# Two hybrid attention layers: latent norms folded into weights and evictions, panels reordered, modulation moved out of the first panels

## The chip, the core and the metric

The kernel runs on one core of a Trainium2 chip. The core has a matrix engine (TensorE, in the profile PE for matmuls and PEld for weight loads), VectorE (DVE), ScalarE (ACT), GpSimd (POOL) and SyncE (SP, which here only issues transfers). The metric is the device time of one execution in microseconds (us), the median of several runs. Less is better.

## The reference, cut to what matters

512 latent tokens and 256 context tokens pass through two layers of width 1024. Layer 0 has two groups of heads with one input projection: eight multi-head latent attention heads and eight neighbourhood attention heads. Layer 1 has sliding-window attention. Each layer ends in a SwiGLU. What the change touches is in layer 0: the modulated input, the projection, and the latent heads' norms and up-projections.

```python
def rms_norm(x, gain=None):
    xf = x.astype(jnp.float32)
    y = xf * lax.rsqrt(jnp.mean(xf * xf, axis=-1, keepdims=True) + EPS)
    if gain is not None:
        y = y * gain.astype(jnp.float32)
    return y.astype(x.dtype)
...
    def queries(p, rotate):
        q = rms_norm(p[..., :MLA_Q_RANK], q_norm) @ w_q_up
        q = q.reshape(p.shape[0], p.shape[1], MLA_HEADS, MLA_NOPE + MLA_ROPE)
        q_nope, q_rope = q[..., :MLA_NOPE], q[..., MLA_NOPE:]
        if rotate:
            q_rope = axial_rope(q_rope, rows, cols)
        return jnp.einsum('bshn,hcn->bshc', q_nope, w_uk), q_rope

    def keys(p, rotate):
        c_kv = rms_norm(p[..., MLA_Q_RANK:MLA_Q_RANK + MLA_KV_RANK], kv_norm)
        k_rope = p[..., MLA_Q_RANK + MLA_KV_RANK:][:, :, None, :]
...
    def attend(q_lat, q_rope, c_kv, k_rope):
        sc = jnp.einsum('bqhc,bkc->bhqk', q_lat, c_kv) + jnp.einsum('bqhr,bkr->bhqk', q_rope, k_rope)
        p = jax.nn.softmax(sc.astype(jnp.float32) * scale, axis=-1).astype(c_kv.dtype)
        return jnp.einsum('bhqk,bkc->bqhc', p, c_kv)
```

The query latent has rank 256 (two tiles of 128 features), the key and value latent rank 128 (one tile), the rotated key 32 features. Besides, every layer needs six modulation vectors for each of the two streams: the product of a conditioning vector with a 1024 x 6144 matrix.

## The kernel before, in words

Activations lie with features on the 128 partitions and the 768 tokens (512 latent, `LATS`, then 256 context, `CTXS`) along the free axis. Every fp32 matmul is made of three in a rounded format: operands are split into a high part and a remainder (`split`, lines 303 to 309; `load_w`, lines 268 to 275, for weights: L273 is the high part on ScalarE, L274 the remainder on VectorE or GpSimd), and `mm3` (L283 to L285) adds high x high, high x low, low x high.

Layer 0's mixer goes in this order:

- **Start.** The input is normed and modulated, and the value columns of the neighbourhood heads are projected by `start_products` (through `three`, L696 to L698) into six banks of PSUM at once; `put_vs` empties them by 24 small copies (L418 on VectorE, L419 on ScalarE, by turns).
- **First pair's panels.** `projections(pair_panels(0), PG)` computes queries and keys of the first pair of neighbourhood heads: two weight panels of 1024 x 128, each in 8 steps. Results go to whichever of seven banks comes next (`PG`). Between the steps, `bg` takes one modulation step for every second panel step (`DBG = 0.5`), so eight in all. Here `dense[0]` is true, and a modulation tile is done as L204 and L208 on VectorE for the latent stream, and for the context stream as L221 on GpSimd, L222 on ScalarE and L224 and L225 on VectorE. Outside such stretches both streams are done on VectorE (L233, L235).
- **Neighbourhood jobs** (`na_jobs`, run by `attend`): four pairs of heads, three jobs each. A job computes scores (L680, L681), takes row minima with the bias (L490), exponentials (L486), transposes by TensorE (L427), copies (L418, L419) and weighted sums (L480). `finish_pair` (L405 to L410) divides by the sums. Beside the jobs runs a queue of side steps. `STEPS[0] = (6, 8, 14, 5)` is the number of side steps offered in each job of pair 0, 1, 2, 3; `BG[0]` is the number of modulation steps in each job (one everywhere). The side queue first holds `later_panels`: pair 1, pair 2, latent 0, pair 3, latents 1 and 2, rotated key, eight steps each panel, 80 in all; the remainders of these panels' weights are made on GpSimd. Results go to the two banks "d" (`PQ`).
- Before the last pair's jobs the queue is drained, then `latent_norms` (`gained`, lines 785 to 821) and `mla_prepare` join it, 15 steps. `gained` squares the three latent tiles on GpSimd (L795), adds the two query tiles' squares on VectorE (L799), sums over features by TensorE against a column of ones (L802), takes the root on ScalarE (L805) and the reciprocal on VectorE (L806), builds a diagonal matrix (L810), broadcasts it by TensorE against ones (L814) into a row factor in SBUF (L815), scales each latent tile by gain and factor (L818) and splits it. `mla_prepare` loads three up-projection weights (keys and values, rotated queries, plain queries), and makes the up-projections; their evictions are plain copies on ScalarE (L673; `put_rope` and `rope`, L386 and L781, for the rotated queries).
- `latent_operands(h)` builds what head h's scores read: a cleared tile (L946, GpSimd), the rotated key copied in (L949), high part (L952, ScalarE) and remainder (L953, GpSimd), and the rotated query by a transfer.
- **Latent jobs** (`mla_jobs`): eight heads, two jobs each; beside them the up-projections of pairs 1 to 3 and their values, and one modulation step in each job.

The order of instructions on an engine is fixed before the run by a scheduler that takes program order, priorities (side steps stand back by `lower[0]`) and free buffers. Tiles named "p" share eight buffers (score tiles, temporaries, and the latents), "wr" three (weights being loaded, and every fourth score tile), "wh" and "wl" three each.

Of the kernel before, what the change touches and what calls it, by code (L numbers as in the profile page):

```python
# [41 lines left out]
EV = "dr"  # L42
# [7 lines left out]
DBG = 0.5  # L50
# [3 lines left out]
SQ = 1  # L54
# [8 lines left out]
BG = ((1, 1, 1, 1, 1), 4, (1, 0), (0, 0))  # L63
FIRST = 2000
STEPS = ((6, 8, 14, 5), 5, 3)
# [20 lines left out]
def hybrid_kernel(ctx: ExitStack, tc, I, out):  # L86
# [295 lines left out]
    def rope(dst, src, tabs, swap, scale=1.0, tag="b", eng=None):  # L382
# [3 lines left out]
        S.activation(x[:p, LATS], src, AF.Copy, scale=scale)  # L386
# [4 lines left out]
        eng.tensor_tensor(dst, x[:p, LATS], y[:p, LATS], op=ALU.add)  # L391

# [278 lines left out]
    def put(t, rows=P, scale=1.0):  # L671
        def use(src, c):
            S.activation(t[:rows, c], src, AF.Copy, scale=scale)  # L673

        return use
# [100 lines left out]
    def put_rope(t, tabs, swap, rows=P, scale=1.0, tag="b", eng=None):  # L776
        def use(src, c):
            if c is LATS:
                rope(t[:rows, c], src, tabs, swap, scale, tag, eng)
            else:  # L780
                S.activation(t[:rows, c], src, AF.Copy, scale=scale)  # L781

        return use

    def gained(groups):

        d, m = PQ(), NT // P
        n = m * len(groups)
        col = T("sm", [P, 6, 2]).rearrange("p a b -> p (a b)")[:, :n]
        for i, (tiles, _) in enumerate(groups):  # L790
            acc = None
            for t in tiles:
                s = B()
                if SQ:
                    G.tensor_tensor(s, t, t, op=ALU.mult)  # L795
                else:
                    S.activation(s, t, AF.Square)
                if acc is not None:
                    V.tensor_tensor(s, s, acc, op=ALU.add)  # L799
                acc = s  # L800
            for j in range(m):
                PE.matmul(d[:, i * m + j : i * m + j + 1], acc[:, j * P : (j + 1) * P], ones[:, :1], start=True, stop=True)  # L802
        for i, (tiles, _) in enumerate(groups):
            c = slice(i * m, i * m + m)
            S.activation(col[:, c], d[:, c], AF.Sqrt, bias=eps, scale=1.0 / (P * len(tiles)))  # L805
        V.reciprocal(col, col)  # L806
        yield
        for i, (tiles, g0) in enumerate(groups):
            diag, r = B(), B()
            V.tensor_tensor(diag.rearrange("p (a b) -> p a b", b=P), ident.unsqueeze(1).to_broadcast([P, m, P]),  # L810
                            col[:, i * m : i * m + m].unsqueeze(2).to_broadcast([P, m, P]), op=ALU.mult)
            for c in (LATS, CTXS):
                d = PQ()
                PE.matmul(d[:, : c.stop - c.start], ones, diag[:, c], start=True, stop=True)  # L814
                S.copy(r[:, c], d[:, : c.stop - c.start])  # L815
            res = []
            for j, t in enumerate(tiles):
                V.scalar_tensor_tensor(t, t, gains[:, g0 + j : g0 + j + 1], r, op0=ALU.mult, op1=ALU.mult)  # L818
                res.append(split(t, V))
            groups[i] = res  # L820
            yield
# [3 lines left out]
    ON, lat_raw, kr = [], [None] * 3, []  # L825
# [16 lines left out]
    def projections(panels, get):  # L842

        load = lambda x: load_w(x[0], KT, x[1], G if get is PQ else None)
# [6 lines left out]
    def later_panels():  # L851

        def latent(i):
            def use():
                lat_raw[i] = B(tag="p")
                return put(lat_raw[i])
# [16 lines left out]
        return [*pair(1), *pair(2), latent(0), *pair(3), latent(1), latent(2), (I["w_kr"], 32, rotated)]  # L873
# [20 lines left out]
    def latent_norms():  # L894
        groups = [(lat_raw[2:], 2), (lat_raw[:2], 0)]
        yield from gained(groups)
        wu["ckv"], wu["cq"] = groups

# [415 lines left out]
```

## Time and profile before

| | |
|---|---|
| median of 3 runs | 1696.11 us (1693.7 to 1699.89) |
| profiled execution, its own time | 1700.12 us |
| its span, first to last instruction | 1698.3 us |
| mean granted TensorE clock | 0.972 |
| chain that ended last, by engine | PE 83%, DVE 8%, issue 3%, POOL 2%, ACT 1%, DMA 1% |

The profile is one execution. A line such as `L273 ACT CAST wh<-wr` names the source line, engine, operation, and the tiles written and read; behind the bar stand busy time, mean duration in ns, and how long the engine sat idle before such instructions and for whom. A window's row gives the busy time of each engine with the number of instructions, the granted clock, the share of the transfer engines and the rate. Matmul ends are modelled, so a matmul's own duration overlaps the next; the number of matmuls in a stretch tells the pace.

### The profile page before, as it was taken

To read this page: it belongs to the slowest core of one execution; us is meant where nothing else is said; L and a number is where in the kernel's file an instruction comes from. 1 tells how busy PE (TensorE), PEld (TensorE's weight loads), DVE (VectorE), ACT (ScalarE), POOL (GpSimd) and SP (SyncE) were. 2 spreads that over 40 slices of the span, in tenths; PEclk is the share of its full clock that TensorE was granted. 3 is DMA by queue.
4 is the path that set the end of the run, shared out by engine and by line. 5 is a ranking of instruction groups with operands and counts; after the bars stand their busy time and mean duration, and the time that the engine had idled before them with its cause. 6 is when DMAs were issued, how large, how long until landed. Compare 5 with 4: busy or idle time off the path is not lost.

```text
span 1698.3 us, 24504 instructions
## 1 busy us (share of the span) xinstructions
PE 1609.6 (95%) x9442; PEld 1353.6 (80%) x9442; DVE 972.6 (57%) x2012; ACT 671.5 (40%) x1292; POOL 312.3 (18%) x214
## 2 busy tenths in 40 slices
PE   5989987998998999999999999899999999999997
PEld 3678865776687888888888888787879888888887
DVE  4755335879578854664564424678877533343435
ACT  5455334676345431321221223457755422222223
POOL 0322132230153421310000003376003000000002
PEclk8989987999999999999999999899999999999998
DMA  9415321212532432442453213322005223232322
GB/s 344 144 59 160 102 88 56 66 48 77 203 131 99 156 97 84 137 155 87 150 168 113 81 49 118 105 87 88 1 2 175 87 80 119 83 104 81 116 65 88
DMA packets 73228, 180.44 MB, mean 106 GB/s; under 512 B 9108, under 2 KB 13464, under 8 KB 73112
## 3 DMA queue, kind: packets, MB, share of 16 engines
q1 hardware_dynamic: 71960, 177.83, 31.7%
q8 instruction: 74, 1.21, 0.3%
q10 hardware_dynamic: 1152, 1.05, 0.2%
q14 instruction: 42, 0.34, 0.1%
HBM read 170.72 MB, written 4.19 MB: 103 GB/s over the span
## 4 chain that ended last, share of the span: by engine, by line
PE 83%; DVE 8%; issue 3%; POOL 2%; ACT 1%; DMA 1%; SPq 0%; DVEq 0%; POOLq 0%; ACTq 0%
PE pss L283 9%; PE pss L284 9%; PE pss L285 9%; PE psd L283 8%; PE psd L285 8%; PE psd L284 8%; PE pst L285 6%; PE pst L283 6%; PE pst L284 6%; PE pso L480 5%; PE pst L427 3%; PE pss L680 1%; PE pss L681 1%; PE psd L427 1%; DVE p L490 1%
## 5 line engine op out<-in xcount | busy, mean ns | idle before, releaser
L273 ACT CAST wh<-wr 128x1024 fp32r<-128x1024 f32 (+2 forms) x209 | 200.4, 961 | 482.1 <-PE pss L284 158.0
L274 DVE TENSOR_TENSOR wl<-wr,wh 128x1024 fp32r<-128x1024 f32 (+2 forms) x180 | 212.1, 1179 | 170.8 <-ACT wh L273 168.1
L284 PE MATMUL psd<-b,wh 128*128 128x512 f32 (+3 forms) x644 | 226.3, 351 | 0.0
L285 PE MATMUL psd<-b,wl 128*128 128x512 f32 (+2 forms) x604 | 215.1, 356 | 6.4 <-DVE wl L274 6.4
L283 PE MATMUL psd<-b,wh 128*128 128x512 f32 (+2 forms) x604 | 217.6, 361 | 1.4 <-ACT b L386 1.4
L284 PE MATMUL pss<-b,wh 128*128 128x512 f32 (+1 forms) x564 | 193.5, 344 | 0.0
L283 PE MATMUL pss<-b,wh 128*128 128x512 f32 (+1 forms) x516 | 180.5, 351 | 9.9 <-ACT b L419 8.2
L318 POOL TENSOR_TENSOR p<-p,p 128x256 f32<-128x256 f32 (+1 forms) x42 | 45.5, 1084 | 776.4 <-ACT p L315 773.4
L285 PE MATMUL pss<-b,wl 128*128 128x512 f32 (+1 forms) x516 | 179.6, 348 | 0.0
L284 PE MATMUL pst<-b,wh 128*128 128x512 f32 (+1 forms) x392 | 134.4, 343 | 1.0 <-DVE b L352 0.9
L284 PEld LDWEIGHTS psd<-b,wh 128*128 128x128 f32 (+1 forms) x644 | 122.1, 190 | 16.3 <-issue 0.7
L285 PEld LDWEIGHTS psd<-b,wl 128*128 128x128 f32 (+1 forms) x604 | 114.3, 189 | 23.7 <-DVE wl L274 7.2
L283 PEld LDWEIGHTS psd<-b,wh 128*128 128x128 f32 (+1 forms) x604 | 114.6, 190 | 19.4 <-ACT b L386 1.7
L283 PE MATMUL pst<-b,wh 128*128 128x512 f32 (+1 forms) x352 | 122.8, 350 | 2.3 <-ACT wh L273 2.3
L285 PE MATMUL pst<-b,wl 128*128 128x512 f32 (+1 forms) x352 | 122.8, 349 | 1.1 <-DVE wl L274 1.1
L486 ACT ACTIVATE p<-p,sm 128x512 f32<-128x512 f32 (+3 forms) x144 | 105.1, 730 | 35.4 <-DVE sm L490 35.1
L284 PEld LDWEIGHTS pss<-b,wh 128*128 128x128 f32 x564 | 109.2, 194 | 11.5
L283 PEld LDWEIGHTS pss<-b,wh 128*128 128x128 f32 x516 | 100.1, 194 | 22.9 <-ACT b L419 8.6
L285 PEld LDWEIGHTS pss<-b,wl 128*128 128x128 f32 x516 | 100.1, 194 | 11.7
L283 PE MATMUL pss<-st,wh 128*128 128x512 f32 (+1 forms) x286 | 100.1, 350 | 1.9 <-ACT st L307 1.4
L285 PE MATMUL pss<-st,wl 128*128 128x512 f32 (+1 forms) x286 | 99.4, 348 | 0.1
L221 POOL TENSOR_TENSOR ph<-ph,cond 128x512 f32<-128x512 f32 x28 | 47.6, 1699 | 280.0 <-DVE mod L204 215.0
(276 smaller groups left out, 3672.1 us busy)
## 6 DMA issues: line engine op xcount, KB each, us to landing
wr<-in_w_gu_dram SPq DMA_DIRECT2D x88, 512.0 KB, 3.5
wr<-in_w_out_dram SPq DMA_DIRECT2D x32, 512.0 KB, 3.8
ph<-in_mod_w_dram SPq DMA_DIRECT2D x60, 256.0 KB, 4.0
pl<-in_mod_w_dram SPq DMA_DIRECT2D x60, 256.0 KB, 3.8
wr<-in_w_dn_dram SPq DMA_DIRECT2D x40, 320.0 KB, 2.9
wr<-in_w_dn_dram SPq DMA_DIRECT2D x32, 384.0 KB, 3.1
wr<-in_w_in_dram SPq DMA_DIRECT2D x21, 512.0 KB, 3.7
nb<-in_nb_dram SPq DMA_DIRECT2D x16, 384.0 KB, 3.5
```

The source lines that it names most:

```text
L221: G.tensor_tensor(w, w, cond[:, 1, c], op=ALU.mult)
L273: S.copy(h, r)
L274: (G if eng else V).tensor_tensor(lo, r, f(h), op=ALU.subtract)
L283: PE.matmul(o, wh[:, k], mh[:, c], start=first and k == 0, stop=False)
L284: PE.matmul(o, wh[:, k], ml[:, c], start=False, stop=False)
L285: PE.matmul(o, wl[:, k], mh[:, c], start=False, stop=last and k == n - 1)
L318: (eng or V).tensor_tensor(acc[:, :n], acc[:, :n], t[:, :n], op=ALU.add)
L427: ins = PE.transpose(o[:, i * P : (i + 1) * P], b, ident)
L480: ins = PE.matmul(o[64 * i : 64 * i + 64, c], v(kt), t, start=n == 0, stop=n == len(moving[i]) - 1)
L486: S.activation(p[:, c], p[:, c], AF.Exp, bias=nm, scale=-1.0, accum_out=dn)
L490: V.tensor_tensor_reduce(out=p[:, c], in0=s, in1=bias, op0=ALU.add, op1=ALU.min, scale=-1.0, scalar=start, accum_out=nm)
L680: PE.matmul(o, x, ks[0][:, keys], start=True, stop=False)
```

## The change

1. **Norms.** The gain of each latent feature is multiplied into the up-projection weights as they are loaded (`load_gained`: the high part on ScalarE with a scale, the remainder on VectorE). The latents are split unscaled. Their squares are made by ScalarE from the same bank as the latent itself; `factors` builds the row factor once for the key and value latent and once for the query latent, and the evictions of the up-projections multiply by it on VectorE (`scaled`, and in `values` by the factor as a column).
2. **Order.** The later panels come as pairs 1, 2, 3, rotated key, latent 2, latent 0, latent 1. `mla_prepare` stands in the side queue right behind them, without a drain, in 14 steps. `STEPS[0]` becomes (7, 9, 11, 6).
3. **Modulation.** No modulation step is taken beside the first pair's panels; jobs of the first three pairs take two each instead of one.
4. **Engines.** The later panels' weight remainders, and for the first two latent heads the remainders ("l") and the clearing of tiles ("z"), move from GpSimd to VectorE.

```diff
-EV = "dr"
+EV = "dlrz"
-DBG = 0.5
-SQ = 1
-BG = ((1, 1, 1, 1, 1), 4, (1, 0), (0, 0))
+BG = ((2, 2, 2, 1, 1), 4, (1, 0), (0, 0))
-STEPS = ((6, 8, 14, 5), 5, 3)
+STEPS = ((7, 9, 11, 6), 5, 3)
...
         x, y = B(tag=tag), B(tag=tag)
-        S.activation(x[:p, LATS], src, AF.Copy, scale=scale)
+        scaled(x, src, LATS, scale)
...
+    def scaled(t, src, c, scale):
+
+        p = src.shape[0]
+        if isinstance(scale, float):
+            S.activation(t[:p, c], src, AF.Copy, scale=scale)
+        else:
+            V.tensor_tensor(t[:p, c], src, scale[:p, c], op=ALU.mult)
...
-    def gained(groups):
+    def factors(square, nfeat, scale):
 
         d, m = PQ(), NT // P
...
+        for j in range(m):
+            PE.matmul(d[:, j : j + 1], square[:, j * P : (j + 1) * P], ones[:, :1], start=True, stop=True)
+        S.activation(col, d[:, :m], AF.Sqrt, bias=eps, scale=1.0 / nfeat)
         V.reciprocal(col, col)
...
+        diag, r = B(), B(tag="p")
+        V.tensor_tensor(diag.rearrange("p (a b) -> p a b", b=P), ident.unsqueeze(1).to_broadcast([P, m, P]),
+                        col.unsqueeze(2).to_broadcast([P, m, P]), op=ALU.mult)
+        for c in (LATS, CTXS):
+            d = PQ()
+            PE.matmul(d[:, : c.stop - c.start], ones, diag[:, c], start=True, stop=True)
+            S.activation(r[:, c], d[:, : c.stop - c.start], AF.Copy, scale=scale)
+        return col, r
+
+    def load_gained(src, m, gain):
+
+        r, h, lo = T("wr", [P, 2 * m]), T("wh", [P, 2 * m], F32R), T("wl", [P, 2 * m], F32R)
+        dma(r, src)
+        for k in range(2):
+            c, g = slice(k * m, k * m + m), gains[:, gain[k] : gain[k] + 1]
+            S.activation(h[:, c], r[:, c], AF.Copy, scale=g)
+            V.scalar_tensor_tensor(lo[:, c], r[:, c], g, f(h[:, c]), op0=ALU.mult, op1=ALU.subtract)
+        return tuple(x.rearrange("p (k m) -> p k m", k=2) for x in (h, lo))
...
-        load = lambda x: load_w(x[0], KT, x[1], G if get is PQ else None)
+        load = lambda x: load_w(x[0], KT, x[1])
...
             def use():
-                lat_raw[i] = B(tag="p")
-                return put(lat_raw[i])
+                lat[i], square = (B(tag="b" if i == 1 else "p") for _ in range(2))
+
+                def put(src, c):
+                    S.copy(lat[i][:, c], src)
+                    S.activation(square[:, c], src, AF.Square)
+                    if i == 1:
+                        V.tensor_tensor(squares[0][:, c], squares[0][:, c], square[:, c], op=ALU.add)
+
+                squares[i] = square
+                return put
...
-        return [*pair(1), *pair(2), latent(0), *pair(3), latent(1), latent(2), (I["w_kr"], 32, rotated)]
+        return [*pair(1), *pair(2), *pair(3), (I["w_kr"], 32, rotated), latent(2), latent(0), latent(1)]
...
     def mla_prepare():
-        wu["kv"] = load_w(I["w_ukv"], 2, 512, G)
-        w = load_w(I["w_qr"], 2, 256, G)
-        wu["qn"] = load_w(I["w_qn"], 2, 512, G)
+        wu["kv"] = load_gained(I["w_ukv"], 512, (2, 2))
+        w = load_gained(I["w_qr"], 256, (0, 1))
+        wu["qn"] = load_gained(I["w_qn"], 512, (0, 1))
+        wu["rk"] = factors(squares[2], P, 1.0)
+        yield
+        wu["rq"] = factors(squares[0], 2 * P, MLA_SCALE)
+        yield
+        wu["ckv"] = [split(lat[2], V)]
+        wu["cq"] = [split(lat[0], V), split(lat[1], V)]
+        yield
         KR.extend(split(kr[0][:32, :NT], V))
-        yield
-        yield from pair_ups(0)
         for i in range(2):
             t = B()
-            yield from up(cut(w, i * P, P), wu["cq"], put_rope(t, rope0, SWAP8, scale=MLA_SCALE, eng=V if "r" in EV and i == 0 else None))
+            yield from up(cut(w, i * P, P), wu["cq"], put_rope(t, rope0, SWAP8, scale=wu["rq"][1], eng=V if "r" in EV and i == 0 else None))
             QR.append(split(t, V))
             if i == 0:
+                yield from pair_ups(0, False)
                 ready.append(latent_operands(0))
-
-    def pair_ups(p):
+        yield from values(0)
+
+    def pair_ups(p, also=True):
         kn.append(B())
         qn.append(B())
         wk = wu["kv"]
-        yield from up(cut((wk[0][:, 0:1], wk[1][:, 0:1]), p * P, P), wu["ckv"], put(kn[p]))
-        yield from up(cut(wu["qn"], p * P, P), wu["cq"], put(qn[p], scale=MLA_SCALE))
-        if p % 2 == VP:
+        yield from up(cut((wk[0][:, 0:1], wk[1][:, 0:1]), p * P, P), wu["ckv"], put(kn[p], scale=wu["rk"][1]))
+        yield from up(cut(wu["qn"], p * P, P), wu["cq"], put(qn[p], scale=wu["rq"][1]))
+        if also and p % 2 == VP:
             yield from values(p - VP)
...
-                copy(VM[p + j][:, t * P : (t + 2) * P].rearrange("p (t c) -> p t c", c=P),
-                     o.rearrange("p (t j c) -> p t j c", t=2, j=2)[:, :, j])
+                V.tensor_tensor(VM[p + j][:, t * P : (t + 2) * P].rearrange("p (t c) -> p t c", c=P),
+                                o.rearrange("p (t j c) -> p t j c", t=2, j=2)[:, :, j],
+                                wu["rk"][0][:, t : t + 2].unsqueeze(2).to_broadcast([P, 2, P]), op=ALU.mult)
...
                 lower[0] = L3
-                drain()
-                beside(latent_norms())
-                beside(mla_prepare())
...
-    i = 0
     for _ in projections(pair_panels(0), PG):
-        i += 1
-        bg(int(i * DBG) - int(i * DBG - DBG))
+        pass
     dense[0] = False
     beside(projections(later_panels(), PQ))
+    beside(mla_prepare())
     attend(na_jobs())
```

44 lines of the change are left out of this document (4 added, 40 removed).

## The prediction

> **What bounds the kernel now.** I read the page first: the totals, then the slices of the span.
>
> ```profile
> span 1698.3 us, 24504 instructions
> PE 1609.6 (95%) x9442; PEld 1353.6 (80%) x9442; DVE 972.6 (57%) x2012; ACT 671.5 (40%) x1292; POOL 312.3 (18%) x214
> ...
> PE   5989987998998999999999999899999999999997
> ...
> PEclk8989987999999999999999999899999999999998
> ```
>
> TensorE is the engine that sets the time. The change only touches the first quarter of the span, and there the slices (42.5 us each) show two places where TensorE is less busy and granted a lower clock: the third slice (85 to 127 us) and the sixth and seventh (212 to 297 us). The first slice is the start, which the change leaves alone. So I next asked for the busy time by stage: the end of the start products, the first pair's panels, the neighbourhood jobs with panels beside them, the stretch where the latents are normed, and the latent-attention jobs. Columns: TensorE, weight loads, VectorE, ScalarE, GpSimd busy (instructions), granted clock, DMA share, GB/s.
>
> ```profile
> 58.00:76.00 18.00, 17.49 (x83) 13.89 (x83) 17.04 (x31) 9.96 (x21) 7.24 (x5) 1.00 0.43 138
> 76.00:95.00 19.00, 10.80 (x50) 9.48 (x49) 17.52 (x42) 6.33 (x18) 13.48 (x11) 0.73 0.25 84
> 100.00:226.00 126.00, 124.96 (x852) 106.83 (x852) 57.37 (x145) 60.91 (x138) 22.05 (x13) 1.00 0.38 116
> 226.00:312.00 86.00, 70.19 (x408) 50.57 (x407) 47.97 (x92) 35.71 (x79) 25.05 (x18) 0.80 0.20 64
> 312.00:412.00 100.00, 96.97 (x690) 75.39 (x689) 84.55 (x242) 70.08 (x157) 24.37 (x14) 1.00 0.15 48
> ```
>
> Matmuls per time tell more than busy time. The jobs at 100 to 226 us issue one per 148 ns, the latent jobs at 312 to 412 us one per 145 ns, the valley at 226 to 312 us one per 211 ns with the clock at 0.80. In the panels' stretch, 50 matmuls take 19 us (380 ns each) where the stretch before needs 217 ns for matmuls of the same width. These two stretches are all that the change can win.
>
> **The first pair's panels.** The chain of waits runs over VectorE here; the waits of TensorE in 58 to 100 us have one large entry, and VectorE's groups in 58 to 95 us show what stood in its queue.
>
> ```profile
> PE pss L283 <- ACT b L419: 8.2, 1, 8.2
> ```
> ```profile
> L208 DVE SCALAR_TENSOR_TENSOR mod<-mod,modb 128x1 f32<-128x1 f32 x4 | 3.8, 956 | 0.0
> ...
> L233 DVE CUSTOM_DVE_ANT_0 pl<-wr,cond 128x1024 bf16<-128x1024 f32 x2 | 3.5, 1754 | 0.0
> L274 DVE TENSOR_TENSOR wl<-wr,wh 128x1024 fp32r<-128x1024 f32 x2 | 3.3, 1653 | 0.0
> L204 DVE CUSTOM_DVE_ANT_0 p<-pl,cond,mod 128x512 bf16<-128x512 f32 x4 | 3.0, 738 | 0.0
> L204 DVE CUSTOM_DVE_ANT_0 p<-ph,cond 128x512 bf16<-128x512 f32 x4 | 2.7, 680 | 0.0
> L418 DVE COPY b<-pss 128x128 f32<-128x128 f32 x8 | 2.0, 276 | 0.0
> L224 DVE TENSOR_TENSOR mod<-part,part 128x1 f32<-128x1 f32 x4 | 1.9, 474 | 0.0
> ```
>
> TensorE waits 8.2 us for a panel's bank: all banks still hold value products, and the copies that empty them (L418, L419) queue behind the eight modulation steps (four tiles, both vectors). Without these, L208, both L204 groups and L224 go: 3.8 + 3.0 + 2.7 + 1.9 = 11.4 us out of 34.6 us of VectorE's work in 58 to 95 us, and eight GpSimd products with them. The wait of 8.2 us is shorter than the 11.4 us that leave ahead of it. At 217 ns the 50 matmuls need 10.8 us instead of 19, a gain of 8.2, which also contains the lost clock (0.73). What could eat it: the L233 pair in this list is the first jobs' modulation, already put here; each of these jobs now draws two steps, so two more may come (two at 1.75 us, 3.5 us). So this term lies between 5 and 9; I take 8, nearest the wait that it removes.
>
> **The valley.** Its waits of TensorE, then VectorE's groups of 226 to 312 us, and three pieces of the timeline:
>
> ```profile
> PE pss L680 <- DVE sm L490: 4.7, 1, 4.7
> PE pst L409 <- DVE b L410: 4.2, 1, 4.2
> ```
> ```profile
> L949 DVE CAST st<-b 32x768 fp32r<-32x768 f32 x4 | 8.0, 2036 | 0.1
> L799 DVE TENSOR_TENSOR b<-b,b 128x768 f32<-128x768 f32 x1 | 5.0, 4951 | 0.0
> ...
> L818 DVE SCALAR_TENSOR_TENSOR p<-p,mla_gain,b 128x768 f32<-128x768 f32 x3 | 3.0, 1015 | 5.5 <-ACT b L815 5.5
> L308 DVE TENSOR_TENSOR b<-p,b 128x768 fp32r<-128x768 f32 x3 | 2.9, 958 | 0.9 <-ACT b L307 0.9
> L410 DVE TENSOR_TENSOR b<-b,pst 128x512 f32<-128x512 f32 x4 | 2.8, 688 | 3.5 <-PE pst L409 3.5
> ...
> L810 DVE TENSOR_TENSOR b<-ident_r,sm 128x768 f32<-128x768 f32 x2 | 1.9, 954 | 0.0
> ...
> L410 DVE TENSOR_TENSOR b<-b,pst 128x256 f32<-128x256 f32 x3 | 1.3, 418 | 2.6 <-PE pst L409 2.6
> ```
> ```profile
> 234.38 4.95 DVE L799 TENSOR_TENSOR b<-b,b 128x768 f32<-128x768 f32 x1
> ...
> 273.83 1.02 DVE L949 CAST st<-b 32x768 fp32r<-32x768 f32 x2
> ...
> 281.49 6.98 DVE L949 CAST st<-b 32x768 fp32r<-32x768 f32 x2
> ```
> ```profile
> 236.18 2.33 POOL L274 TENSOR_TENSOR wl<-wr,wh 128x1024 fp32r<-128x1024 f32 x1
> ...
> 283.22 2.76 POOL L946 MEMSET st<- 32x768 f32 x4
> 286.06 4.10 POOL L953 TENSOR_TENSOR st<-b,st 64x768 fp32r<-64x768 f32 x2
> ```
>
> Two things are late. First, one VectorE sum takes 4.95 us where another of its form (L308) takes 0.96, and two casts take 6.98 us where two others took 1.02; beside both runs GpSimd work. TensorE's two waits, 4.2 and 4.7 us, end behind exactly these. The Trainium skill (SBUF — State Buffer, Who interferes with whom) says that VectorE and GpSimd share one port pair, held by one instruction while the other fully blocks; these rows agree. The change takes the work off GpSimd here: squares are made by ScalarE as a panel's bank is emptied, weight remainders (L274) by VectorE, the first pair's remainders and the clearing of tiles (L953, L946) by VectorE.
>
> Second, the order. Now all panels are drained, then the norms run as a chain (squares, sum, reciprocal root, diagonal, broadcast, scaling L818, split L308), and only then the first up-projections. So TensorE has only attention to do, and the clock falls. After the change the latents are split unscaled, the up-projections need no norm, and only their evictions wait for the factor. The counts fit: panels take 80 steps, and 3 x 7 + 3 x 9 + 3 x 11 = 81 are given before the last pair's jobs; preparing takes 14 steps, of which 13 fall among 18 offered in the last three jobs (before: 15 of 15). TensorE's work is the same.
>
> At the latent jobs' 145 ns the valley's 408 matmuls need 59 us: a gain of 27 is the upper end. The lower end is the two waits, 4.2 + 4.7 = 9: contention gone, order worth nothing. Against the upper end stand two factor chains that are now built separately:
>
> ```profile
> L805 ACT ACT_TABLE_LOAD x1 | 1.3, 1283 | 0.0
> ...
> L815 ACT COPY b<-psd 128x512 f32<-128x512 f32 x2 | 1.2, 585 | 4.3 <-PE psd L814 4.3
> ```
>
> Each holds a table load (1.28), the diagonal (L810, 0.95) and the broadcast's eviction (0.59): 2.8 us, 5.6 for both if nothing covers them. While an eviction waits on VectorE, the score minima and copies queued behind it wait, and TensorE for its bank. So I take 27 - 5 = 22. A rule that speaks against the change: the Trainium skill (ScalarE: Activation LUTs, What ACT_TABLE_LOAD costs) adds a drain, 2.66 us for each switch; the trace here shows 1.28 for the load. By it two bare chains would cost 8.4 instead of 5.6 and the valley's gain would be 19.
>
> **What is added elsewhere.** Nine panels' remainders move from GpSimd to VectorE, and nine more modulation steps fall in the first nine jobs:
>
> ```profile
> L274 POOL TENSOR_TENSOR wl<-wr,wh 128x1024 fp32r<-128x1024 f32 x8 | 19.1, 2387 | 91.1 <-ACT wh L273 59.9 <-PE pss L680 31.1
> ```
> ```profile
> L233 DVE CUSTOM_DVE_ANT_0 pl<-wr,cond 128x1024 bf16<-128x1024 f32 x6 | 7.6, 1272 | 2.5 <-DMA wr<-in_mod_w_dram 2.5
> ```
> ```profile
> L274 DVE TENSOR_TENSOR wl<-wr,wh 128x1024 fp32r<-128x1024 f32 (+2 forms) x180 | 212.1, 1179 | 170.8 <-ACT wh L273 168.1
> ```
>
> That is 9 x 1.27 + 9 x 1.18 = 22 us for VectorE, whose 57.4 us of 126 become about 79: TensorE, busy 125 of 126, still hides it. The bound is the 2.5 us that such a step already waits for its weights on SyncE's queue; three buffers of that kind serve panels, modulation and every fourth score tile. I take 0.
>
> In the latent jobs, twelve evictions (six of 512, six of 256 columns) go from ScalarE to VectorE. The nearest row is L410, also a product that reads a bank: 6 x 0.69 + 6 x 0.42 = 6.6 us on an engine busy 84.55 of 100. That gives about 91 beside TensorE's 97. Cover is thin: between 0 and 6.6, I take 3. A gain is excluded: the busier engine takes work from the less busy one.
>
> Sum: -8 - 22 + 0 + 3 = -27 us against the profiled execution's own 1700.12, so 1673. The median is 1696.11, 4 below it; the forecast is 1696 - 27 = 1669.
>
> **The rivals.** (1) The valley is the last pair's own latency: three jobs with light steps beside them cannot fill TensorE whatever the order of the norms. Then the valley gives only what the later stages take back, and the panels' 8 less 3 remain: 1691. For it: the attention's own matmuls are all that fills the valley. Against it: the latent jobs have the same kind of chain and run at 145 ns. (2) Slower: score tiles. Pool "p" has 8 buffers. The change keeps the rotated key, two latents and two squares there, and then two factor tiles until the last up-projection. Latent jobs in flight hold two and four score tiles, of which at least one is elsewhere, so five of the six left. If one more were missing, a job's scores could not start before the previous job's transposes, and sixteen jobs would each show their softmax:
>
> ```profile
> L490 DVE CUSTOM_DVE_ANT_0 p<-pss,zeros,sm 128x512 f32<-128x512 f32 x23 | 16.9, 745 | 7.6 <-PE pss L964 7.6
> ...
> L418 DVE COPY ph<-pst 128x512 f32<-128x512 f32 x14 | 9.4, 683 | 0.4 <-PE pst L427 0.3
> ```
> ```profile
> L486 ACT ACTIVATE p<-p,sm 128x768 f32<-128x768 f32 (+1 forms) x37 | 28.5, 771 | 8.7 <-DVE sm L490 8.6
> ```
>
> 0.75 + 0.77 + 0.68 = 2.2 us, twice for the two halves of a tile's scores: up to 4.4 x 16 = 70, at half of that 35, against 27 gained: 1704 to 1739, say 1715. It decides from the seventh live tile on. (3) The modulation does not leave: its steps, now in the jobs, are put ahead of the value copies as the L233 pair is. Then the first term is 0 to 3 and VectorE stays the bound there: 1696 - 22 + 3 = 1677, or 1674 with 3. With the valley at its lower end as well, 1690.
>
> **How the numbers follow.** A measurement of this kernel tells 0.5% (8.5 us) from no change. Forecast as written: 0.60. Third rival, still faster: 0.16, of which 0.04 lands within 8.5 us. First rival: 0.12, a quarter of it faster by more. Second: 0.12, of which 0.03 is hidden enough to land within 0.5%. So faster 0.60 + 0.12 + 0.03 = 0.75, same 0.04 + 0.09 + 0.03 = 0.16, slower 0.09. Low end: -9 - 27 + 0 = -36, 1660, and 4 for stretched VectorE work that also ends elsewhere: 1656. High end: the first rival, 1691. Outside lie the second rival and a part of the first, under 0.2.
>
> **What would show it.** Right: no wait of TensorE over 2 us before 95 us, clock 1.00 there; the summed squares and the casts near 1 us; the valley's matmuls at about 160 ns and its clock above 0.9; VectorE near 90% in the latent jobs. Wrong: a stretch after the last panel still at half clock, TensorE waiting on evictions of the up-projections, or latent jobs longer than 106 us.

## The result, and the profile after

The changed kernel takes 1673.45 us (median of 4 runs, 1673.07 to 1675.31); the kernel before, measured beside it, took 1695.49. The ratio is 0.9868, with a 95% interval of 0.9848 to 0.9889: 22 us less. The profiled execution took 1673.2 us (span 1671.4, mean clock 0.979).

First the page of the changed kernel: totals, and the slices of TensorE and of its clock.

```profile
span 1671.4 us, 24451 instructions
...
PE 1599.5 (96%) x9442; PEld 1345.7 (81%) x9442; DVE 983.1 (59%) x2056; ACT 661.8 (40%) x1259; POOL 248.2 (15%) x178
...
PE   5999998999999999999999999899999999999997
...
PEclk8999997999999999999999999999999999999999
```

The dip in the third slice is gone; the sixth and seventh, once 8 and 7, are 9 and 8, and the clock of the seventh is still 7. Next the stages, with the prediction's bounds (engine columns as there: TensorE, weight loads, VectorE, ScalarE, GpSimd, clock, DMA share, GB/s).

```profile
58.00:76.00 18.00, 17.52 (x84) 13.90 (x83) 12.71 (x25) 7.53 (x13) 0.00 (x0) 1.00 0.39 137
76.00:95.00 19.00, 19.00 (x108) 16.69 (x107) 12.74 (x34) 7.57 (x17) 4.34 (x6) 1.00 0.25 85
100.00:226.00 126.00, 123.96 (x847) 103.35 (x847) 70.66 (x167) 59.46 (x139) 4.62 (x5) 0.99 0.46 144
226.00:312.00 86.00, 72.33 (x452) 54.12 (x450) 65.98 (x161) 44.27 (x91) 10.01 (x6) 0.86 0.20 62
312.00:412.00 100.00, 96.34 (x660) 72.02 (x661) 88.83 (x242) 62.01 (x136) 17.78 (x9) 0.97 0.22 74
```

The second row is what was hoped for: 108 matmuls where 50 were, at full clock. The fourth is not. The valley has 452 matmuls instead of 408, one per 190 ns instead of 211, and a clock of 0.86 instead of 0.80; the prediction expected 160 ns and over 0.9. At the latent jobs' 145 ns, 452 matmuls would take 65.5 us, so 20.5 us are still lost there, against 26.8 before. The valley gave 6 us of the 22 that were forecast.

So the time must have come from elsewhere too. The trace tells where, by events that both kernels have: the first score of the neighbourhood jobs starts at 99.2 us instead of 108.9 (9.6 earlier); the last latent weighted sum ends at 426.2 instead of 442.4 (16.1 earlier, so 6.5 more); the first SiLU of layer 0's SwiGLU, with the load of its table, starts at 514.3 instead of 535.1 (20.8 earlier, so 4.7 more). These last 4.7 us lie in the output projection, which the prediction didn't speak of. Behind that point the code is the same, and both kernels need 487.6 us from the first to the last SiLU of layer 0. Layer 1, with the same code, took 669.5 us after the change and 675.6 before it; over all kernels of this study it spreads from 669 to 676. At least a part of that is no edit's doing: e10, shown below, has the changed kernel's order of instructions in layer 1 on all four engines, and took 673.0. The profiled execution before was 4.6 us above its median, so the 26.9 us between the two spans are more than the change gave; 20.8 agrees with the 22 of the medians.

What is late in the valley now? TensorE's waits in 226 to 312 us:

```profile
PE pst L411 <- DVE ph L424: 3.1, 1, 3.1
PE psd L174 <- DVE b L397: 2.2, 1, 2.2
...
PE psd L804 <- DVE b L800: 0.9, 1, 0.9
PE psd L281 <- DVE b L397: 0.8, 1, 0.8
```

All four lines shown end behind VectorE, two that are left out between them (1.0 and 0.9 us) behind ScalarE. L397 is the eviction times the factor, L800 the diagonal of `factors`; L424 is a copy, and the timeline of VectorE shows what stood ahead of it:

```profile
267.33 1.50 DVE L953 MEMSET st<- 32x768 f32 x2
268.77 0.62 DVE L496 CUSTOM_DVE_ANT_0 p<-pss,nb 128x512 f32<-128x512 f32 x1
...
269.50 1.51 DVE L953 MEMSET st<- 32x768 f32 x2
271.02 1.02 DVE L956 CAST st<-b 32x768 fp32r<-32x768 f32 x2
...
272.08 0.72 DVE L385 STREAM_SHUFFLE b<-b 128x512 f32<-128x512 f32 x1
272.69 0.67 DVE L424 COPY ph<-pst 128x512 f32<-128x512 f32 x1
```

The clearing of tiles that came from GpSimd (L953, 0.75 us each) stands there, then the key's copies. The kernel before put 47.97 us of work on VectorE in this window, this one 65.98. The old waits went, and VectorE's own queue gave new ones. The granted clock tells the same: it was 0.50 in 239.1 to 245.8, 256.2 to 262.8 and 273.3 to 283.3 us, so the prediction's sign against itself, "a stretch after the last panel still at half clock", is there.

### The profile page after: what moved, and what is told of

Same layout as the page of the kernel before. It is cut to its first block, busy times and chain, and to the rows that moved or that the text cites. A ratio compares the mean times of both kernels' runs of the same rounds, so it can differ in the third digit from the quotient of the medians.

```text
span 1671.4 us, 24451 instructions
## 1 busy us (share of the span) xinstructions
PE 1599.5 (96%) x9442; PEld 1345.7 (81%) x9442; DVE 983.1 (59%) x2056; ACT 661.8 (40%) x1259; POOL 248.2 (15%) x178
## 5 line engine op out<-in xcount | busy, mean ns | idle before, releaser
L271 ACT CAST wh<-wr 128x1024 fp32r<-128x1024 f32 (+3 forms) x206 | 197.8, 962 | 477.5 <-PE pss L282 151.9
L272 DVE TENSOR_TENSOR wl<-wr,wh 128x1024 fp32r<-128x1024 f32 (+2 forms) x190 | 222.7, 1174 | 184.1 <-ACT wh L271 179.9
L282 PE MATMUL psd<-b,wh 128*128 128x512 f32 (+2 forms) x644 | 224.8, 349 | 0.0
L281 PE MATMUL psd<-b,wh 128*128 128x512 f32 (+2 forms) x604 | 215.9, 358 | 0.8 <-DVE b L397 0.8
L316 POOL TENSOR_TENSOR p<-p,p 128x256 f32<-128x256 f32 (+1 forms) x42 | 44.9, 1070 | 777.4 <-ACT p L313 774.4
L283 PE MATMUL pst<-b,wl 128*128 128x512 f32 (+1 forms) x352 | 122.7, 348 | 1.9 <-POOL wl L272 1.9
L281 PE MATMUL pss<-st,wh 128*128 128x512 f32 (+1 forms) x286 | 99.4, 348 | 2.2 <-ACT st L305 1.8
L282 PE MATMUL pss<-st,wh 128*128 128x512 f32 (+1 forms) x238 | 85.3, 359 | 0.0
```

The lines of the kernel that those rows point to most:

```text
L271: S.copy(h, r)
L272: (G if eng else V).tensor_tensor(lo, r, f(h), op=ALU.subtract)
L281: PE.matmul(o, wh[:, k], mh[:, c], start=first and k == 0, stop=False)
L282: PE.matmul(o, wh[:, k], ml[:, c], start=False, stop=False)
L283: PE.matmul(o, wl[:, k], mh[:, c], start=False, stop=last and k == n - 1)
L316: (eng or V).tensor_tensor(acc[:, :n], acc[:, :n], t[:, :n], op=ALU.add)
```

## The experiments

The table has each kernel's median, its ratio to the kernel before, measured beside it (95% interval), and the matmuls in 226 to 312 us (ns for each; granted clock). The last two columns are stretches of its profile, in us: "jobs" from the first neighbourhood score to the end of the last latent weighted sum, "output" from there to the first SiLU.

| kernel | us | ratio | matmuls, ns, clock | jobs | output |
|---|---|---|---|---|---|
| before | 1695.49 | 1 | 408, 211, 0.80 | 333.5 | 92.7 |
| after | 1673.45 | 0.9868 (0.9848 to 0.9889) | 452, 190, 0.86 | 327.0 | 88.0 |
| e1_mod_only | 1684.69 | 0.9928 (0.9912 to 0.9944) | 412, 209, 0.80 | 334.7 | 87.5 |
| e2_no_mod | 1684.25 | 0.9932 (0.9912 to 0.9952) | 470, 183, 0.86 | 325.7 | 93.9 |
| e3_ev_dr | 1677.1 | 0.9911 (0.9879 to 0.9943) | 460, 187, 0.86 | 327.9 | 87.5 |
| e4_pool_lo | 1674.0 | 0.9867 (0.9847 to 0.9888) | 443, 194, 0.86 | 327.2 | 87.5 |
| e5_36_steps | 1685.56 | 0.9944 (0.9926 to 0.9963) | 444, 194, 0.86 | 329.8 | 94.2 |
| e6_no_factor | 1661.08 | 0.9801 (0.9777 to 0.9825) | 517, 166, 0.92 | 311.1 | 87.5 |
| e7_even_steps | 1677.16 | 0.9898 (0.9876 to 0.9920) | 424, 203, 0.86 | 326.9 | 87.4 |
| e8_old_order | 1676.68 | 0.9893 (0.9868 to 0.9918) | 445, 193, 0.88 | 326.7 | 88.1 |
| e9_const_tile | 1671.74 | 0.9854 (0.9838 to 0.9871) | 486, 177, 0.88 | 316.3 | 88.4 |
| e10_one_root | 1670.82 | 0.9849 (0.9833 to 0.9864) | 498, 173, 0.92 | 320.9 | 87.4 |
| e11_no_mod_wout | 1675.13 | 0.9879 (0.9865 to 0.9894) | 452, 190, 0.86 | 323.6 | 86.0 |
| e12_best | 1675.37 | 0.9883 (0.9861 to 0.9904) | 479, 180, 0.90 | 322.9 | 88.3 |

How much do these stretches differ when nothing was changed in them? The start is left out because it differs by itself: up to the 151st matmul all 14 kernels have the same order on TensorE, and that matmul starts between 42.7 us (e12) and 49.0 us (e9). In 20 to 45 us the clock of e12 is 0.93, that of e9 0.66. A time counted from the start of the profile, such as that of the first SiLU, carries this spread. In the jobs, e11 and the changed kernel have the same order on all engines and differ by 3.4 us; nearly 3 of these arise near 128 us, where TensorE waits for a transfer (1.7 us in the changed kernel, 0.4 in e11), and in the changed kernel the clock falls behind it (0.84 in 130 to 140 us). So in the jobs a difference under 3.4 us tells nothing. From the 1281st matmul on (about 225 us) to the last latent weighted sum these two agree to 0.7 us, 201.7 and 201.0.

**Taking the change apart: e1 and e2.** The first is the kernel before with the modulation moved; the second the changed kernel with the modulation put back.

```diff
-DBG = 0.5
+DBG = 0
-BG = ((1, 1, 1, 1, 1), 4, (1, 0), (0, 0))
+BG = ((2, 2, 2, 1, 1), 4, (1, 0), (0, 0))
```

> The kernel before with the modulation moved alone (none beside the first pair's panels, two steps in each of the first nine jobs). If the first panels' gain comes from the modulation steps that stood ahead of the value copies, the first neighbourhood score comes about 9 us earlier than 109.0 us and the run ends 8 to 10 us below the kernel before, near 1686. Rival, that the gain of that stretch needs the panel remainders off GpSimd as well: at most 5 us, 1690 or more.

```diff
-BG = ((2, 2, 2, 1, 1), 4, (1, 0), (0, 0))
+BG = ((1, 1, 1, 1, 1), 4, (1, 0), (0, 0))
...
     for _ in projections(pair_panels(0), PG):
-        pass
+        i += 1
+        bg(int(i * 0.5) - int(i * 0.5 - 0.5))
```

> The changed kernel with the modulation steps put back beside the first pair's panels and one step in each job. If the parts add, it stands 9 to 10 us above the changed kernel, near 1683, and 12 below the kernel before. If the valley's gain depends on the modulation being elsewhere, the distance to the kernel before shrinks below 8 us.

Moving the modulation alone gave 11.5 us, and all the rest alone 12: the two halves add up to the 22 that were measured (to within the intervals of about 3 us). The modulation was to bring 8 and brought 11.5. From the 151st matmul to the first score, the kernel before needs 63.8 us, e2 61.3, and all kernels without modulation steps there 53.2, so the panels gave 10.6. The output projection comes on top: 87.5 us in e1 and 88.0 in the changed kernel, against 92.7 before and 93.9 in e2. The jobs became no faster in e1. The rest, which was to bring 19, brought 12 by the medians and 7.8 in the jobs.

**The output projection: e5 and e11.** The kernels with the short output projection have taken 37 modulation steps by then, before it and e2 have taken 36. In e5 one of the latent jobs takes no step, so that 36 remain; in e11 the output projection takes none of its own.

```diff
-BG = ((2, 2, 2, 1, 1), 4, (1, 0), (0, 0))
+BG = ((2, 2, 2, 1, 0.95), 4, (1, 0), (0, 0))
```

> The changed kernel with 15 instead of 16 modulation steps beside the latent jobs, so that 36 instead of 37 are done before the output projection, as in the kernel before. Theory: the 5 to 7 us that the changed kernel gains between the last latent score and the first SiLU come from this alignment (which step's GpSimd product falls beside the norm behind the output projection), so it is 4 to 7 us slower than the changed kernel, 1677 to 1680. Rival, that this gain only follows from the earlier end of the jobs: 1672 to 1675.

```diff
-BG = ((2, 2, 2, 1, 1), 4, (1, 0), (0, 0))
+BG = ((2, 2, 2, 1, 1), 4, (0, 0), (0, 0))
```

> The changed kernel without modulation steps beside the output projection of layer 0; they fall to the first feed-forward chunk, where four come with each tile. One step more or less ahead of that projection moved its end by 6 us, so if GpSimd's and VectorE's modulation products beside the projection and its norm are what costs there, leaving them out gives 1 to 6 us more, 1667 to 1672. If it was only which instruction fell where, no difference within 2 us of 1673; if the first chunk then waits for its modulation, slower.

One step less ahead of it makes the output projection 94.2 us long, about what it was before. The kernel is 12 us slower by the medians, 8.3 by the two profiles; that is more than the 6.2 us of this stretch, and what the other executions lost besides isn't shown. Taking all steps out of the output projection (e11) shortens it by 2.1 us more and gives nothing in the end (1.7 slower; its layer 1 took 674.9 us, within that layer's spread). So it isn't the amount of work. The waits of TensorE in e5 have one for the summed squares of the next norm, and the timeline of its VectorE shows the queue ahead of that sum:

```profile
PE pss L326 <- DVE p L316: 4.1, 1, 4.1
```
```profile
469.24 0.74 DVE L1050 SCALAR_TENSOR_TENSOR b<-pss,mod,b 128x512 f32<-128x512 f32 x1
471.30 1.57 DVE L222 TENSOR_TENSOR mod<-part,part 128x1 f32<-128x1 f32 x1 [1.31 <-ACT pl L220]
472.89 2.31 DVE L223 SCALAR_TENSOR_TENSOR mod<-mod,modb 128x1 f32<-128x1 f32 x1
475.13 0.68 DVE L316 TENSOR_TENSOR p<-p,p 128x512 f32<-128x512 f32 x1
```

The same wait in the changed kernel, and its VectorE's timeline:

```profile
PE pss L326 <- DVE p L316: 1.2, 1, 1.2
```
```profile
468.35 0.68 DVE L202 CUSTOM_DVE_ANT_0 p<-ph,cond 128x512 bf16<-128x512 f32 x1
...
469.13 2.69 DVE L316 TENSOR_TENSOR p<-p,p 128x512 f32<-128x512 f32 x1
471.74 1.75 DVE L202 CUSTOM_DVE_ANT_0 p<-pl,cond,mod 128x512 bf16<-128x512 f32 x1
```

In e5 the last sum of squares (L316) stands behind the end of a modulation tile's context half: L222 waits for ScalarE, and L223, an instruction on one element per partition that takes 0.16 us elsewhere, takes 2.31. In the changed kernel the sum comes ahead of both. The kernel before has the same order as e5 (L224 at 485.81, L225 for 2.31 us, the sum at 489.64) and the same wait of 4.2 us; e2 has it with 5.7. In all kernels with 37 steps it is 0.9 to 1.2. The wait's 2.9 us more in e5 are about half of the 6.2; where the rest lies isn't shown. This part of the gain, 4.7 us, came with item 3 of the change by where its count of steps ended.

**The engines: e3 and e4.** e3 gives the remainders and the clearing of the first latent heads' tiles back to GpSimd; e4 gives the later panels' weight remainders back.

```diff
-EV = "dlrz"
+EV = "dr"
```

> The changed kernel with the first two heads' remainders and the clearing of tiles back on GpSimd. Theory of the prediction, that GpSimd's work there holds VectorE up: casts of the rotated key near 3.5 us each again and 4 to 9 us slower than the changed kernel, 1678 to 1682. Rival, that VectorE is now the engine the valley waits for and these moves only loaded it (four clearings of 0.75 us and four remainders of 0.95 us, 6.8 us): 1 to 5 us faster, 1669 to 1672.

```diff
-        load = lambda x: load_w(x[0], KT, x[1])
+        load = lambda x: load_w(x[0], KT, x[1], G if get is PQ else None)
```

> The changed kernel with the later panels' weight remainders back on GpSimd. Theory of the prediction: VectorE hides them among the jobs, so nothing is lost by either place but for contention, 1673 to 1676. Rival, that VectorE at 65 to 80% of these jobs already delays score minima: up to 4 us faster, 1669 to 1672.

e3 is 3.6 us slower by the medians, with an interval that also holds no difference, and its jobs are only 0.9 us longer. What it tells for certain is in the casts of the rotated key, VectorE's group in 226 to 312 us, here of e3:

```profile
L956 DVE CAST st<-b 32x768 fp32r<-32x768 f32 x4 | 7.6, 1932 | 0.1
```

and here of the changed kernel:

```profile
L956 DVE CAST st<-b 32x768 fp32r<-32x768 f32 x4 | 2.0, 547 | 0.0
```

The same instruction takes 3.5 times as long when GpSimd makes remainders and clears tiles beside it (in e3 from 268.69 to 277.4 us, the slow casts from 269.18 to 275.74). The Trainium skill (SBUF — State Buffer, Who interferes with whom) has the two engines share a port pair, which the one that issues first holds for its whole instruction; these rows agree. e3 moves remainders and clearing together and doesn't part them. A long wait of TensorE is back with it, 4.5 us ahead of the first latent score:

```profile
PE pss L969 <- issue: 4.5, 1, 4.5
```

Yet from the 1281st matmul to the last latent sum e3 needs 202.4 us against 201.7. So this contention cost VectorE 5.6 us and the kernel little or nothing: without it, VectorE has 4.2 us of clearing (six of L953 at 0.70) and the remainders to do. In e4 the median and the jobs are the changed kernel's: nine panels' remainders may stand on either engine, as the prediction's 0 said.

**The order: e7 and e8.** e7 gives the last pair's jobs nine side steps instead of six, as the first rival would want them; e8 takes the old order of panels, the old steps and the drain, but keeps the folded norms.

```diff
-STEPS = ((7, 9, 11, 6), 5, 3)
+STEPS = ((7, 8, 8, 9), 5, 3)
```

> The changed kernel with 7, 8, 8, 9 side steps in the jobs of the four pairs instead of 7, 9, 11, 6, so that 11 of the latents' 24 panel steps fall beside the last pair's jobs. If the last pair's jobs lack dense work for TensorE (the first rival of the prediction), 4 to 8 us faster than the changed kernel, 1665 to 1669. If the preparation's own chain is what is late, it starts later and the run is 3 to 10 us slower, 1676 to 1683.

```diff
-STEPS = ((7, 9, 11, 6), 5, 3)
+STEPS = ((6, 8, 14, 5), 5, 3)
-        return [*pair(1), *pair(2), *pair(3), (I["w_kr"], 32, rotated), latent(2), latent(0), latent(1)]
+        return [*pair(1), *pair(2), latent(0), *pair(3), latent(1), latent(2), (I["w_kr"], 32, rotated)]
...
+                drain()
+                beside(mla_prepare())
...
-    beside(mla_prepare())
```

> The changed kernel with the panels in the order before, 6, 8, 14, 5 side steps, and the queue drained before the last pair's jobs and the preparation put in only then; norms stay folded. Theory of the prediction, that most of the valley's gain is the order: 6 to 12 us slower than the changed kernel, 1679 to 1685. Rival, that folding alone gives the gain: 1672 to 1676.

More steps beside the last pair didn't make it faster (3.7 us slower by the medians, with intervals that overlap, and the same jobs), so a lack of steps there isn't what is left of the valley. The old order cost 3.2 us by the medians, again with overlapping intervals, and nothing in the jobs: 326.7 us against 327.0. So the order of panels and the drain, item 2, gave nothing that these runs can show. No kernel folds the norms alone, with the old order and the old engines; that the jobs' gain comes from the folding is what is left when e3, e4 and e8 each take something else back and lose almost nothing.

**The factors: e6, e9, e10 and e12.** e6 leaves the norms' factors out of the result: no chains, and evictions by ScalarE with a constant. e9 leaves them out too, but keeps the evictions on VectorE, as products with a constant tile. e10 computes the reference: one Sqrt and one reciprocal for both factors, by adding the small constant on VectorE.

```diff
-        wu["rk"] = factors(squares[2], P, 1.0)
...
-        wu["rq"] = factors(squares[0], 2 * P, MLA_SCALE)
...
-put(kn[p], scale=wu["rk"][1]))
+put(kn[p]))
-put(qn[p], scale=wu["rq"][1]))
+put(qn[p], scale=MLA_SCALE))
```

> The changed kernel without the two row factors (no sum over features, root, reciprocal, diagonal, broadcast), the up-projections evicted by ScalarE with a constant: the norms' factors are left out of the result. If the two factor chains and the evictions on VectorE hold the valley up, 8 to 15 us faster than the changed kernel, 1658 to 1665. If VectorE's other work (splits, clearing, copies) or the short supply of work for TensorE holds it up, 0 to 4 us faster, 1669 to 1673.

```diff
-        d, m = PQ(), NT // P
...
-            S.activation(r[:, c], d[:, : c.stop - c.start], AF.Copy, scale=scale)
+        V.memset(col, 1.0)
+        V.memset(r, scale)
```

> The changed kernel in which the row factors are constants written once: no sum, root, reciprocal, diagonal or broadcast, but the up-projections are still evicted on VectorE by a product with a tile. The norms' factors are left out of the result. The run without factors and with ScalarE's evictions was 12 us faster than the changed kernel. If the wait for the factor chain was what cost, this one is 9 to 12 us faster too, 1661 to 1664. If the evictions on VectorE were what cost, it is 0 to 4 us faster, 1669 to 1673.

```diff
-        S.activation(col, d[:, :m], AF.Sqrt, bias=eps, scale=1.0 / nfeat)
-        V.reciprocal(col, col)
+            V.tensor_scalar(cols[:, i * m : i * m + m], d[:, :m], 1.0 / nfeat, EPS, op0=ALU.mult, op1=ALU.add)
+        S.activation(cols, cols, AF.Sqrt)
+        V.reciprocal(cols, cols)
```

> The changed kernel with one root for both factors: means and epsilon on VectorE, one Sqrt and one reciprocal for twelve columns, so that ScalarE switches its table to the root and back once instead of twice (2.6 us less of loads), while the first factor has to wait for the last latent. If the switches are on the path: 2 to 4 us faster than the changed kernel, 1669 to 1671. If the chain's matmuls and VectorE's steps are, no difference within 2 us.

e6 is what the prediction had counted on. The row of its valley, from 226 to 312 us, columns as above:

```profile
226.00:312.00 86.00, 75.94 (x517) 58.00 (x516) 68.25 (x181) 52.55 (x119) 11.97 (x8) 0.92 0.22 67
```

The same row of e9:

```profile
226.00:312.00 86.00, 74.27 (x486) 55.75 (x486) 72.04 (x183) 42.44 (x96) 12.50 (x8) 0.88 0.22 67
```

And of e10:

```profile
226.00:312.00 86.00, 75.15 (x498) 56.21 (x497) 70.94 (x176) 43.73 (x93) 11.81 (x9) 0.92 0.22 67
```

Without the factors there are 517 matmuls, 166 ns each, at a clock of 0.92: close to the 160 ns and 0.9 that the prediction named as its sign. The kernel is 12.4 us faster than the changed one, by intervals that don't touch. A window fixed in time holds another part of the work in each kernel, so here is the stretch from the 1281st matmul to the last latent sum, first of the changed kernel, then of e6, e9 and e10:

```profile
224.60:426.20 201.60, 184.27 (x1211) 138.26 (x1210) 159.93 (x406) 110.70 (x235) 28.19 (x16) 0.92 0.22 75
```
```profile
225.80:412.90 187.10, 171.72 (x1179) 129.67 (x1178) 144.85 (x378) 113.72 (x249) 26.91 (x16) 0.95 0.25 80
```
```profile
226.00:418.50 192.50, 176.81 (x1179) 132.12 (x1178) 157.88 (x404) 103.12 (x225) 28.26 (x16) 0.93 0.24 78
```
```profile
226.10:421.10 195.00, 180.53 (x1212) 135.52 (x1210) 159.30 (x407) 107.43 (x232) 27.48 (x17) 0.95 0.24 77
```

The kernel before needs 209.7 us for it. Against the changed kernel, e6 saves 14.6 us, of which e9, which drops the chains alone, has 9.2; the other 5.4 are the evictions' place on VectorE rather than ScalarE (a fill of 0.70 us that e9 adds on VectorE is in them). One root instead of two (e10) saves 6.7. Two things stand beside this. e6 and e9 also leave out the 32 matmuls of the factors themselves (L796 and L804, together about 7 us of TensorE's busy time in the changed kernel), which the kernel before has as well; so their gain isn't waiting alone, while e10 has all of them. And VectorE is as busy in e9 and e10 as in the changed kernel, 157.9 and 159.3 us against 159.9. So what these two gain doesn't come from less work on VectorE. What two roots cost can be read from ScalarE's timeline in the changed kernel:

```profile
228.47 1.28 ACT L797 ACT_TABLE_LOAD   x1
229.76 0.27 ACT L797 ACTIVATE sm<-psd,eps 128x6 f32<-128x6 f32 x1
...
236.48 1.28 ACT L492 ACT_TABLE_LOAD   x1
237.78 0.51 ACT L492 ACTIVATE p<-p,sm 128x256 f32<-128x256 f32 x1
...
238.39 1.28 ACT L797 ACT_TABLE_LOAD   x1
239.69 0.27 ACT L797 ACTIVATE sm<-psd,eps 128x6 f32<-128x6 f32 x1
239.97 1.28 ACT L492 ACT_TABLE_LOAD   x1
```

The second root comes between two exponentials of the same job, so ScalarE loads a table four times, 5.1 us in all; in e10, as in the kernel before, it loads two. Each load is 1.28 us, and the next activation starts 0.01 to 0.02 us behind it. The Trainium skill (ScalarE: Activation LUTs, What ACT_TABLE_LOAD costs) adds a drain to every switch, 2.66 us together; these rows show no such drain. That e10 saved more than its two loads means that part of it is the rest of the second chain, or the order in the queues; no run parts the two.

By the medians the gains of e9 and e10 are smaller, 1.7 and 2.6 us, and their intervals overlap that of the changed kernel. In both profiles layer 1, unchanged, took longer than in the changed kernel's (676.0 and 673.0 us against 669.5 from layer 0's last SiLU to the end), in e10 with the same order of instructions. e12 puts e10 and e4 together:

> The changed kernel with one Sqrt for both factors (2.6 us below the changed kernel when alone) and the later panels' weight remainders on GpSimd again (no difference when alone). Theory that VectorE's queue in the stretch from 225 to 300 us is what is left of the valley: taking the panels' remainders off VectorE does nothing there, since the panels' weights are prepared earlier, so the two give what the one root gave: 1669 to 1673 us. Rival, that VectorE's total in the neighbourhood jobs counts as well: with 10 us less of it the first SiLU comes 3 us or more earlier still and the time is below 1668. Rival, that results of this size come from how steps fall beside one another and don't add: 1674 or above.

Its jobs took 322.9 us, not less than those of e10, and layer 1 took 676.3 us: 1675.37 in all, so the second theory, that the two add up, is not borne out, and the total lies where the third had it. In the stretch from the 1281st matmul the profiles of e10 and e12 are earlier than the changed kernel's (195.0 and 197.1 us against 201.7), but the medians show no gain, so no version that certainly beats the changed kernel can be named; e10 has the lowest median among those that compute the reference.

## Why the prediction was right, and where it was not

The forecast was 1669 us with a range from 1656 to 1691; 1673.45 was measured, 4.4 us above. Direction and size were right. That the total came so near is partly luck, as the steps of the sum show:

- **First pair's panels, -8.** Measured: 10.6 from the 151st matmul to the first score. The sign was as named: full clock, and no wait of TensorE over 0.5 us in 58 to 100 us. e1 shows that it is the modulation alone: it needs the same 53.2 us there. The third rival, that the steps come back ahead of the value copies, did not happen.
- **The valley, -22.** Measured: 6.3 by the pace of the matmuls in the window, and 8.0 from the 1281st matmul to the last latent sum (209.7 to 201.7), which holds the latent jobs too. This step failed, where it took 27 - 5 = 22, near its upper end. Two things were wrong in it. The price of the factors was too low: each chain was given one table load, where two chains need four in the changed kernel, and the evictions' place on VectorE was priced in the latent jobs alone, with 3. Against these 5 + 3 = 8 stand the 14.6 us of e6, of which e10 wins back 6.7 by one root less; a part of the 14.6 is the factors' own matmuls. With the factors gone altogether, their matmuls too, e6 comes to 22.6 us less than before: even so not to the upper end of 27. And the order, which the prediction made the second of its two causes, can be taken back without loss (e8). The contention went as told: the casts took 547 ns, and the summed squares (now L857) 0.69 and 0.42 us for their two halves where one sum had taken 4.95. But the lower end of 9, contention alone, was too high as well: e3 has the slow casts back and loses 0.7 us in that stretch. The sign "TensorE waiting on evictions of the up-projections", named as one against the forecast, is there: L397, 2.2 and 0.8 us.
- **Added work beside the first jobs, 0.** Nearly right: 847 matmuls in 126 us where there were 852, with VectorE at 70.7 us instead of 57.4 (79 was expected). From the first score to the 1281st matmul the changed kernel needs 125.3 us instead of 123.8; one wait of TensorE for a transfer stands there, 0.6 us long before, but e11 with the same order needs 122.7.

```profile
PE pss L687 <- DMA st<-st: 1.7, 1, 1.7
```

- **Evictions in the latent jobs, +3.** Too much for the latent jobs themselves. Up to the last latent score the window's row is

```profile
300.00:397.00 97.00, 94.87 (x682) 72.42 (x681) 87.43 (x247) 60.66 (x142) 17.78 (x9) 1.00 0.14 45
```

  VectorE is busy for 90%, as was said, and TensorE still makes a matmul per 142 ns, against 145 before. The 5.4 us between e6 and e9 are what these evictions cost in valley and latent jobs together. (The sign "longer than 106 us" can't be read any more: the first latent score now starts at 269.7 us, inside the valley.)
- **Not in the sum, -4.7.** In the output projection the count of modulation steps decides which instruction stands ahead of the last sum of squares. The prediction counted the steps that item 3 takes away and adds, eight less and nine more, and didn't follow them to the end, where the difference of one stands.

So from the first score to the last latent sum 6.5 us came where 22 - 3 = 19 were forecast, 12.5 too few, and the panels' 2.6 more and the output projection's 4.7 made up for over half of that (the start took 0.9 us longer): 20.8 instead of 27. The 4.7 us were luck, since nobody had counted on them. The first rival named the right place, that little would come of the valley, with the wrong reason: e7 shows that it isn't steps that TensorE lacks beside the last pair, and e6 that the valley fills better when the factors are gone. The second rival, a score tile short in the latent jobs, would show in them, and TensorE is busy there for 98%. The third was refuted with the panels.

## What to carry to other kernels

In a stage in which TensorE is starved, a wait that is taken away gives its length only if nothing else holds the stage: here slow casts and a wait of 4.5 us came back (e3), and the stretch became 0.7 us longer. Price a new chain by every step that it adds, the way back too: a root between two exponentials costs two table loads, and one root less won 6.7 us in its stretch, though the medians don't show it beyond their intervals. Folding a norm into evictions turns copies, which any engine can make, into products which here VectorE made, and that was over a third of what the factors cost. When side steps are moved, follow their count to the stage where they run out, since one step more can set which instruction stands ahead of the last one of a chain. And before two profiles are compared by a point in time, look for a stretch whose instructions are the same in both, and see how much it differs by itself.

## What the runs showed of the hardware

- A 128 x 1 instruction on VectorE (L223, 0.16 us elsewhere) took 2.31 us in the output projection, and a 128 x 512 sum (L316) 2.69 us instead of 0.68, in stretches in which GpSimd was subtracting weight remainders (L272).
- Clearing 32 x 768 in fp32 takes VectorE 0.70 us (six of L953), more than a copying cast of the same size when GpSimd does nothing beside it (547 ns).
- The granted clock in the valley was 0.86, with stretches at 0.50, although the longest single wait of TensorE there was 3.1 us.
- The same order of matmuls up to the 151st ended its start between 42.7 and 49.0 us, with a clock of 0.93 and 0.66 in 20 to 45 us at the two ends.
